# Loading the last 384 rows of three batches as fp32 through the SyncE queue beside the casting GpSimd queue

## The chip, the cores and the metric

One core of one Trainium2 chip. The metric is device time in microseconds, the median of several executions.

In the lines of the profile PE is TensorE, PEld its loading of weights, DVE VectorE, ACT ScalarE, POOL GpSimd and SP SyncE; q0 is the queue of the loads that GpSimd issues, q1 that of SyncE, and L75 is line 75 of the kernel. HBM is the memory outside the core, SBUF the one inside it. The rows "DMA" and "GB/s" cut the span in 40 slices: a digit is the busy share of the 16 DMA engines in tenths (9 is 90% or more), and GB/s is what they wrote.

## The reference

For each of 4 matrices of 4224 x 4224 fp32, the 2D prefix sum, its diagonal, and the running sum along that diagonal:

```python
def reference(x):
    ps = np.cumsum(np.cumsum(x, axis=1), axis=2)
    diag = np.diagonal(ps, axis1=1, axis2=2)
    return np.cumsum(diag, axis=1).astype(np.float32)
```

Every element of x counts, so 285.5 MB have to come from HBM; the result is 67 KB.

## The kernel before

Each batch is read as "strips": five of 768 rows (six rows per partition, `F2 = 6`) and a last one of 384 rows (three per partition, `F = 3`). All are cast from fp32 to bf16 by the load and share a pool of three buffers. The fourth batch cuts its end differently and is not changed.

```python
NBUF = 3
strips = ctx.enter_context(tc.tile_pool(name="strips", bufs=NBUF))

def strip_tile():
    return strips.tile([P, F2, N], BF16, name="strip")

def load_rows(o, b, r0):
    f = o.shape[1]
    nc.gpsimd.dma_start(
        out=o, in_=x[b, r0 : r0 + f * P, :].rearrange("(p f) w -> p f w", f=f))
# ... (cut)
def add_up(strip, f, r0, acc, ums, wp=0, ws=None):
    # TensorE sums the columns right of the diagonal block, straight from the strip
    for j in range(g + nw, NG):
        for q in range(f):
            columns(j, 0, GW, strip[:, q, j * GW : (j + 1) * GW])
    # ... (cut)
    for q in range(f):
        mu = mup.tile([P, F2 * P], BF16, name="mu")[:, : f * P]
        masked(mu, strip[:, q, r0:hi], ums[q], acc[:, q, 2:3])   # VectorE
        for h in range(nw):
            columns(g + h, 0, GW, mu[:, h * GW : (h + 1) * GW])  # TensorE
        if ws > wp:
            act_sum(acc[:, q, 0:1], strip[:, q, wp:ws])          # ScalarE
    row_sums(acc[:, :, 1], strip[:, :, ws:hi])                   # VectorE
# ... (cut) after the six-row strips of a batch:
        strip = strip_tile()
        if whole:                                   # batches 0, 1, 2
            load_rows(strip[:, :F], b, T0)
            add_up(strip[:, :F], F, T0, acc3[:, 0], um3)
```

## Time and profile before

| | before |
|---|---|
| time, median of the first 3 runs | 669.56 us |
| span of the profiled run | 667.0 us |
| busy: PE, VectorE, ScalarE, GpSimd | 32%, 50%, 21%, 4% |
| read from HBM | 285.47 MB, 428 GB/s over the span |
| loads through the GpSimd queue | 142.47 MB written (half of what is read) |

The table is read from the bottom: the two lines about bytes say what the kernel waits for, and the line of busy shares says that no compute engine comes near to that. The lines of the profile that carry this stand in the prediction.

### The profile page before, as it was taken

To read this page: it belongs to the slowest core of one execution; us is meant where nothing else is said; L and a number is where in the kernel's file an instruction comes from. 1 tells how busy PE (TensorE), PEld (TensorE's weight loads), DVE (VectorE), ACT (ScalarE), POOL (GpSimd) and SP (SyncE) were. 2 spreads that over 40 slices of the span, in tenths; PEclk is the share of its full clock that TensorE was granted. 3 is DMA by queue.
4 is the path that set the end of the run, shared out by engine and by line. 5 is a ranking of instruction groups with operands and counts; after the bars stand their busy time and mean duration, and the time that the engine had idled before them with its cause. 6 is when DMAs were issued, how large, how long until landed. Compare 5 with 4: busy or idle time off the path is not lost.

```text
span 667.0 us, 2828 instructions
## 1 busy us (share of the span) xinstructions
PE 215.1 (32%) x967; PEld 97.2 (15%) x967; DVE 336.3 (50%) x376; ACT 140.1 (21%) x225; POOL 27.0 (4%) x56
## 2 busy tenths in 40 slices
PE   0071522403118254140321633504032254250426
PEld 0030211101003022010110311201011122120202
DVE  2043617366924351745883415266398241635687
ACT  0001120406300103040630020304063002030436
POOL 5000000000000000000000000000000000001000
PEclk9995857666558586665655957567565586765758
DMA  9999999999999999999999999999999999999997
GB/s 203 219 219 219 218 219 219 217 217 216 208 215 219 219 219 217 216 219 219 219 219 215 216 211 217 220 219 216 216 216 219 220 215 218 216 215 219 216 207 144
DMA packets 7384, 143.25 MB, mean 215 GB/s; under 512 B 669, under 2 KB 842, under 8 KB 1866
## 3 DMA queue, kind: packets, MB, share of 16 engines
q0 software_dynamic: 7008, 142.47, 99.7%
q1 hardware_dynamic: 362, 0.61, 0.3%
q8 instruction: 7, 0.11, 0.1%
q14 instruction: 7, 0.06, 0.0%
HBM read 285.47 MB, written 0.07 MB: 428 GB/s over the span
## 4 chain that ended last, share of the span: by engine, by line
another core or an unknown queue 42%; DVE 25%; PE 23%; DMA 5%; issue 4%; DVEq 0%; POOLq 0%
PE d L198 23%; DVE acc L215 17%; DVE mu L218 7%; DMA strip<-in_x_dram 5%; PE fold L198 1%; DVE pu L215 0%; DVE c L397 0%; DVE c L218 0%; DVE tsum L215 0%; DVE acc L301 0%; DVE acc L304 0%; PE carry_ps L198 0%; DVE rows L331 0%; DVEq L218 0%
## 5 line engine op out<-in xcount | busy, mean ns | idle before, releaser
L218 DVE SCALAR_TENSOR_TENSOR mu<-strip,um 128x768 bf16<-128x768 bf16 (+1 forms) x129 | 110.7, 908 | 314.4 <-DMA strip<-in_x_dram 222.3
L198 PE MATMUL d<-strip,sel 128*11 128x384 bf16 x603 | 140.0, 406 | 344.4 <-DMA strip<-in_x_dram 344.4
L210 ACT ACTIVATE dump<-strip 128x416 bf16<-128x416 bf16 (+8 forms) x112 | 128.4, 1146 | 523.2 <-DMA strip<-in_x_dram 520.2
L215 DVE TENSOR_REDUCE acc<-strip 128x6 f32<-128x4608 bf16 (+6 forms) x23 | 195.9, 8518 | 0.0
L198 PEld LDWEIGHTS <-sel 128*11 128x11 bf16 x849 | 86.1, 101 | 526.3 <-issue 488.4
L198 PE MATMUL d<-mu,sel 128*11 128x384 bf16 x243 | 59.7, 355 | 67.5 <-DVE mu L218 67.4
L75 POOL DMA_DIRECT2D strip<-in_x_dram x24 | 16.5, 687 | 555.5 <-DVE acc L215 414.5
L210 ACT ACTIVATION_READ_ACCUMULATOR dump<-strip 128x1 f32 x112 | 20.9, 186 | 0.0
L218 DVE DVE_READ_ACCUMULATOR mu<-strip,um 128x1 f32 x129 | 10.6, 82 | 0.0
L198 PE MATMUL d<-ident,rows 128*11 128x128 f32 x24 | 5.2, 378 | 16.5 <-DVE rows L340 16.5
L198 PE MATMUL fold<-strip,ident_h 128*128 128x480 bf16 (+1 forms) x14 | 4.3, 458 | 8.4 <-DMA strip<-in_x_dram 8.4
L198 PE MATMUL d<-halves,rows 128*11 128x64 f32 x48 | 5.7, 304 | 0.0
L198 PEld LDWEIGHTS d<-halves,rows 128*11 128x11 f32 x48 | 5.1, 136 | 2.1 <-issue 2.1
L198 PEld LDWEIGHTS d<-ident,rows 128*11 128x11 f32 x24 | 2.6, 118 | 18.2 <-DVE rows L340 11.5
L215 DVE TENSOR_REDUCE pu<-d 11x1 f32<-11x384 f32 x4 | 2.2, 546 | 5.5 <-PE d L198 5.5
L397 DVE TENSOR_TENSOR_SCAN c<-ones_row,carry,c 11x384 f32<-11x384 f32 x4 | 4.0, 1006 | 0.1
L397 DVE TENSOR_TENSOR_SCAN c<-ones_row,carry,d 11x384 f32<-11x384 f32 x4 | 4.0, 1001 | 0.1
L198 PEld LDWEIGHTS <-ident_h 128*128 128x128 bf16 x20 | 2.2, 112 | 12.2 <-issue 11.8
L215 DVE TENSOR_REDUCE parts<-strip 128x3 f32<-128x3072 bf16 x1 | 3.4, 3350 | 0.0
L198 PE MATMUL d<-hmu,sel 128*11 128x384 bf16 (+2 forms) x3 | 0.7, 286 | 6.7 <-DVE hmu L218 6.7
L372 POOL DMA_DIRECT2D strip<-in_x_dram x2 | 1.4, 716 | 29.2 <-DVE acc L215 29.2
L215 DVE TENSOR_REDUCE tsum<-strip 128x1 f32<-128x384 bf16 (+2 forms) x3 | 1.7, 568 | 0.9 <-DMA strip<-in_x_dram 0.9
(78 smaller groups left out, 36.0 us busy)
## 6 DMA issues: line engine op xcount, KB each, us to landing
strip<-in_x_dram POOLq DMA_DIRECT2D x19, 6336.0 KB, 69.6
strip<-in_x_dram POOLq DMA_DIRECT2D x5, 3168.0 KB, 55.3
strip<-in_x_dram POOLq DMA_DIRECT2D x1, 1080.0 KB, 45.3
strip<-in_x_dram POOLq DMA_DIRECT2D x1, 768.0 KB, 48.2
head<-in_x_dram SPq DMA_DIRECT2D x1, 528.0 KB, 3.9
strip<-in_x_dram POOLq DMA_DIRECT2D x1, 448.0 KB, 51.1
strip<-in_x_dram POOLq DMA_DIRECT2D x1, 416.0 KB, 49.5
strip<-in_x_dram POOLq DMA_DIRECT2D x1, 160.0 KB, 51.4
```

The lines of the kernel that those rows point to most:

```text
L75: nc.gpsimd.dma_start(out=o, in_=x[b, r0 : r0 + f * P, :].rearrange("(p f) w -> p f w", f=f))
L198: nc.tensor.matmul(o, lhsT=lhsT, rhs=rhs, start=start, stop=False, skip_group_check=True)
L210: nc.scalar.activation(out=dump[:, :w], in_=src, func=ACT.Copy, accum_out=acc)
L215: nc.vector.reduce_sum(out=acc, in_=src, axis=AX.X)
L218: nc.vector.scalar_tensor_tensor(out=o, in0=i, scalar=1.0, in1=m, op0=ALU.mult, op1=ALU.mult, accum_out=acc,)
L372: nc.gpsimd.dma_start(out=part_a[:, :, c0:c1], in_=src_a[:, :, c0:c1])
L397: nc.vector.tensor_tensor_scan(out=c12[:, i, :], data0=ones_row, data1=src, initial=carry[:, i : i + 1], op0=ALU.mult, op1=ALU.add,)
```

## The change

A load that doesn't cast can be issued by SyncE, as these three are in the changed kernel. The three-row strip as fp32 has just the size of a six-row strip as bf16, so it fits the same buffers. The intent is to have these three loads run beside the GpSimd queue and not behind it.

```diff
-    def load_rows(o, b, r0):
+    def load_rows(o, b, r0, eng=nc.gpsimd):
         f = o.shape[1]
-        nc.gpsimd.dma_start(
+        eng.dma_start(
@@
-        strip = strip_tile()
         if whole:
-            load_rows(strip[:, :F], b, T0)
-            add_up(strip[:, :F], F, T0, acc3[:, 0], um3)
+            strip = strips.tile([P, F, N], FP32, name="strip")
+            load_rows(strip, b, T0, nc.sync)
+            add_up(strip, F, T0, acc3[:, 0], um3)
@@
         else:
+            strip = strip_tile()
```

## The prediction

> **What bounds the kernel now.** I read first the page's slices and DMA queues, because every strip is loaded from HBM once.
>
> ```profile
> DMA  9999999999999999999999999999999999999997
> GB/s 203 219 219 219 218 219 219 217 217 216 208 215 219 219 219 217 216 219 219 219 219 215 216 211 217 220 219 216 216 216 219 220 215 218 216 215 219 216 207 144
> q0 software_dynamic: 7008, 142.47, 99.7%
> q1 hardware_dynamic: 362, 0.61, 0.3%
> HBM read 285.47 MB, written 0.07 MB: 428 GB/s over the span
> ```
>
> The DMA row is at 9 in 39 of 40 slices: the 16 engines never pause. The GB/s row counts bytes written to SBUF. The GpSimd queue casts fp32 to bf16 on the way, so each byte written stands for two read: 219 GB/s written is 438 read. All of x is read once, 285.5 MB, and at about 434 GB/s that alone takes 658 us of the 667 us span.
>
> The windows view (busy time of PE, PEld, DVE, ACT and POOL with instruction counts, then clock, DMA share, GB/s) shows how idle the rest is:
>
> ```profile
> 100.00:150.00 50.00, 12.53 (x57) 5.43 (x55) 28.51 (x20) 9.81 (x16) 1.26 (x2) 0.66 1.01 218
> 300.00:400.00 100.00, 29.12 (x128) 13.44 (x128) 53.42 (x54) 20.52 (x30) 2.84 (x4) 0.59 1.01 216
> ```
>
> DMA share is 1.01 while VectorE, the busiest engine, is at 53 to 57%. The chain agrees. Its unnamed pieces are the loads that it can't follow:
>
> ```profile
> 125.25 5.72 PE d L198 x20
> ...
> 133.72 11.27 DVE acc L215
> 144.98 10.12 another core or an unknown queue
> ...
> 160.62 13.28 DVE acc L215
> ...
> 176.41 6.58 DVE acc L215
> ...
> 186.66 13.36 another core or an unknown queue
> 200.07 11.71 PE d L198 x56
> ```
>
> Strip 3 (counting from 0) lands at about 125.2 us, where PE starts. VectorE waits again until strip 4 at 155.2. ScalarE starts the three-row strip 5 of batch 0 at 170.14 (timeline), and strip 6, batch 1's first, starts at 200.07. A six-row strip (12.98 MB read) thus takes 29.9 us and a three-row strip (6.49 MB) 15.0, both 433 to 434 GB/s: the spacing of landings is the transfer time.
>
> Last, whether the queue comes near to running dry. GpSimd's timeline has the issues (start, duration, idle before it and what ended that):
>
> ```profile
> 115.10 0.56 POOL L75 DMA_DIRECT2D strip<-in_x_dram  x1 [30.14 <-DVE acc L215]
> 145.61 0.70 POOL L75 DMA_DIRECT2D strip<-in_x_dram  x1 [29.95 <-DVE acc L215]
> 174.52 0.72 POOL L75 DMA_DIRECT2D strip<-in_x_dram  x1 [28.21 <-DVE acc L304]
> 183.51 0.72 POOL L75 DMA_DIRECT2D strip<-in_x_dram  x1 [8.27 <-issue]
> 219.92 0.71 POOL L75 DMA_DIRECT2D strip<-in_x_dram  x1 [35.70 <-DVE acc L215]
> ```
>
> These are strips 5 to 9, each issued when the strip three before it has been used up (three buffers). At 145.6 the queue still holds work until 170.1, at 174.5 until 200.0: some 25 us of transfers are always waiting.
>
> **What the Trainium skill says.** "DMA: Bandwidth & Descriptors", Where 436 GB/s comes from: the ceiling is 16 SBUF ports of 32 B at 850 MHz, 435 GB/s, so 27.2 per engine. The trace agrees: in its packet records a cast packet of 25,344 B written (50,688 read) takes 1,886 ns and the next on that engine starts 1,867 ns after it, 27.15 GB/s of bytes read. The same page, Issuing engines are not separate DMA queues: transfers issued by SyncE and GpSimd run on the same 16 engines and interleave, and several issuers save only issue time. The trace before has no two large queues at once to test it. The same page, Queues, rings and completion order: each engine takes turns between the queues that have work, packet by packet; also untested here. "VectorE: DVE Perf Modes", The perf-mode tier table: tensor_reduce runs at 1x in bf16 and fp32 alike. The groups by form agree:
>
> ```profile
> L215 DVE TENSOR_REDUCE acc<-strip 128x3 f32<-128x6240 bf16 x3 | 19.9, 6647 | 0.0
> L218 DVE SCALAR_TENSOR_TENSOR mu<-strip,um 128x384 bf16<-128x384 bf16 x15 | 7.6, 554 | 1.8 <-DMA strip<-in_x_dram 1.7
> L215 DVE TENSOR_REDUCE hs<-head 128x2 f32<-128x1056 f32 x1 | 1.2, 1202 | 0.0
> L218 DVE SCALAR_TENSOR_TENSOR hmu<-head,um 128x384 bf16<-128x384 f32 x1 | 0.5, 534 | 0.0
> ```
>
> 6647 ns over 6240 bf16 elements is 1.07 ns each; 1202 over 1056 fp32 elements is 1.14 including the fixed part. The masked product of 384 columns took 554 ns from bf16 and 534 from fp32.
>
> **The change part by part.** *Bytes.* Three loads (batches 0 to 2) leave the casting queue. What is read from HBM is unchanged; what is written for them doubles, 9.73 to 19.46 MB (3 x 128 partitions x 50,688 B). Now they take 3 x 15.0 = 45 us of DMA time, 6.8% of the total. Does an uncast byte cost more? Cast packets fit 22 ns plus bytes read over 27.2 per ns: 286 ns for 7,168 read, 340 for 8,640, 1,886 for 50,688. The uncast packets in the same trace follow that line too: the runtime's 8,192 B packets have a median of 322 ns (the line gives 323), the 2,112 B packets of the SyncE-loaded head 86 (line: 100). So the engine's time goes by bytes read, and the three loads should keep 3 x 15 us: 0 us of change.
>
> *Issue.* GpSimd loses 3 of its 24 strip issues, about 0.7 us each; it is 4% busy and issues 25 us ahead: 0 us.
>
> *Compute.* On a three-row last strip (batches 0 to 2) there are three masked products, three ScalarE sums of 2,144 columns (1990 ns from bf16; no fp32 one exists in the trace) and one reduce of 6,240. No matmul reads the strip itself, since no column group lies right of it; PE reads only the bf16 product. By the pairs above VectorE stays at about 8.3 us per strip. If ScalarE stays at its rate too, 0 us; even a doubling would add 6 us to an engine that is 21% busy.
>
> *Order.* This is what really moves. Strip 5 is issued at 115.1 as before, but no longer stands behind strips 3 (10 us left) and 4 (30 us). With equal turns strip 3 lands near 135 instead of 125, strip 5 near 145 instead of 170, and strip 4 near 170 instead of 155; the sum, 10 + 30 + 15 us, ends at 170 either way. Strip 3's buffer then comes free 20 us after its landing, so strip 6 is issued near 156 (145.6 before) with 14 us of work still queued. Strip 4 is used up near 189, so strip 7 is issued near 190 (174.5 before) with strip 6 streaming until 200: 10 us left, the tightest point. Then VectorE does strip 5 (about 9 us) and the batch's end (5 us) by about 204, so strip 6 starts some 2 to 4 us late and strip 9 is issued near 223, with strip 7 and all of 8 ahead of it. The engines never run dry and the delay is gone before the next batch ends. 0 us.
>
> *End.* The last batch is untouched: the last load lands at about 661.3 us and 5.7 us of tail follow.
>
> Sum: 0 us, so 669.5.
>
> **The rivals.** First, uncast writes cost more. If an engine's time went by bytes written, the 45 us would double: about 714. If by read plus written (6 B per element cast, 8 uncast), a third more: +15, about 684. For it: no uncast packet of tens of KB has been seen, and its writes need the full 27.2 GB/s of a port that cast packets half use. Against: the 8,192 B packets on the same line. A small penalty of 5% would be +2 us, and I leave room for that.
>
> Second, the change of order starves the queue. If strip 3 or 4 landed so late that its successor was issued into an empty queue, each batch would lose the gap. For it: slack falls from 25 to 10 us by my schedule. Against: 10 us is still left, and it hardly depends on how turns are shared, since even if SyncE's transfer went wholly first, strip 3 would land at 140, strip 6 be issued at 160, and strip 4 still land at 170. A loss of up to 5 us per batch would make about 685 in the worst case.
>
> Third, two queues side by side fill holes and it gets faster. Packets on an engine already follow with 1,867 ns start to start against 1,863.5 at 27.2 GB/s, and dips such as slice 11's 208 GB/s add up to a few us, only a part of them near these loads: at best -3 us, about 666.
>
> **How the range and the chances follow.** All terms are zero because the bound resource moves the same bytes read at the same rate. The unknown is the large uncast packet (0 to +3 us likely, +15 unlikely) and the starvation (0 likely); on the other side at most -3. So 669.5, with 8 in 10 between 665 and 675. 2% is 13.4 us: gaining that would need more than the ceiling allows; losing it needs the first or second rival nearly in full.
>
> **What would show it.** Right: span near 667, HBM read 285.47 MB, q1 at about 20.1 MB and q0 at 132.7, DMA still 9 in every slice but the last, the GB/s row up (towards 330) in the slices where both queues run, SyncE's three loads landing some 30 us after issue, before the six-row strip issued ahead of them, and GpSimd issues for the next batch's first strips some 10 to 15 us later against the landings. The fp32 reduce stays near 6.6 us. Wrong: a slice with DMA under 9 (starvation), or full DMA with a later end (uncast packets slower than 15 us per strip), or a 6,240-element reduce or ScalarE sum much longer and strips waiting on it.

## The result, and the profile after

The changed kernel took 670.92 us (669.74 to 671.73, 6 runs), the kernel before 669.67 (668.67 to 670.19, 6 runs). The ratio is 1.0019, with an interval of 1.0006 to 1.0032. Within 2% this is the same time; whether the 1.25 us are real is the first question of the experiments.

The page of the changed kernel, the lines that answer to those in the prediction (its profiled run, 671.73 us, was the slowest of the six):

```profile
DMA  9999999999999999999999999999999999999995
GB/s 200 218 216 218 217 218 218 339 291 218 218 218 218 216 218 215 224 333 278 218 216 218 220 216 218 218 241 339 263 216 216 220 218 217 216 216 218 218 204 113
q0 software_dynamic: 6576, 132.74, 92.5%
q1 hardware_dynamic: 794, 20.07, 7.1%
HBM read 285.47 MB, written 0.07 MB: 426 GB/s over the span
```

DMA is at 9 in 39 of 40 slices, as before. q1, SyncE's queue, rose from 0.61 to 20.07 MB. The GB/s row has three new peaks of 333 to 339, one per changed load: there half of the engines' turns write 4 bytes per element and not 2. More is written, nothing more is read, and the DMA engines were and are busy throughout. A 9 could hide a gap of a tenth of a slice, 1.7 us; the packet records show none: between 6 and 655 us of both profiled runs all 16 engines always have a packet.

The order did change. The timelines of SyncE, GpSimd and PE (start, duration, and in brackets the idle time before) around the end of batch 0:

```profile
114.65 0.36 SPq L75 DMA_DIRECT2D strip<-in_x_dram  x1
```

```profile
153.01 0.71 POOL L75 DMA_DIRECT2D strip<-in_x_dram  x1 [65.85 <-DVE acc L215]
190.18 0.71 POOL L75 DMA_DIRECT2D strip<-in_x_dram  x1 [36.46 <-DVE acc L304]
199.17 0.71 POOL L75 DMA_DIRECT2D strip<-in_x_dram  x1 [8.27 <-DVE acc L304]
222.60 0.72 POOL L75 DMA_DIRECT2D strip<-in_x_dram  x1 [22.72 <-DVE acc L215]
```

```profile
133.43 4.60 PE L198 MATMUL d<-strip,sel 128*11 128x384 bf16 x18 [27.47 <-DMA strip<-in_x_dram]
170.80 2.08 PE L198 MATMUL d<-strip,sel 128*11 128x384 bf16 x6 [29.15 <-DMA strip<-in_x_dram]
202.25 11.86 PE L198 MATMUL d<-strip,sel 128*11 128x384 bf16 x54
```

SyncE issues strip 5 at 114.65. PE gets strip 3 at 133.4 (125.2 before) and strip 4 at 170.8 (155.2 before). In the packet records the data of strip 5 run from 118.0 to 146.6 us (its last completion is at 148.5), before strip 4, although strip 4 was issued 28 us earlier; on each engine one 50,688 B packet of SyncE's alternates with one of GpSimd's, each about 1,885 ns. Strips 6 and 7 are issued at 153.0 and 190.2 (145.6 and 174.5 before). Then the delay melts: PE begins strip 6 at 202.25, 2.2 us later than before, and strip 9 is issued 2.7 us later.

Compute cost nothing. The groups by form, the ScalarE sum before, which the prediction had not shown:

```profile
L210 ACT ACTIVATE dump<-strip 128x2144 bf16<-128x2144 bf16 x9 | 17.9, 1990 | 13.4 <-DMA strip<-in_x_dram 13.2
```

and after, all three kinds of work that now read fp32:

```profile
L215 DVE TENSOR_REDUCE acc<-strip 128x3 f32<-128x6240 f32 x3 | 19.9, 6647 | 0.0
L210 ACT ACTIVATE dump<-strip 128x2144 bf16<-128x2144 f32 x9 | 17.9, 1990 | 0.3
L218 DVE SCALAR_TENSOR_TENSOR mu<-strip,um 128x384 bf16<-128x384 f32 x9 | 4.5, 555 | 0.1
```

6647, 1990 and 555 ns against 6647, 1990 and 554: equal to a nanosecond. The idle time before the ScalarE sums fell from 13.4 to 0.3 us, because the strip is there early; ScalarE is no bottleneck, so this is worth nothing.

### The profile page after: what moved, and what is told of

Same layout as the page of the kernel before. It is cut to its first block, busy times and chain, and to the rows that moved or that the text cites. A ratio compares the mean times of both kernels' runs of the same rounds, so it can differ in the third digit from the quotient of the medians.

```text
span 670.0 us, 2832 instructions
## 1 busy us (share of the span) xinstructions
PE 216.2 (32%) x967; PEld 97.5 (15%) x967; DVE 336.1 (50%) x376; ACT 140.1 (21%) x225; POOL 25.3 (4%) x53
## 3 DMA queue, kind: packets, MB, share of 16 engines
q1 hardware_dynamic: 794, 20.07, 7.1%
## 4 chain that ended last, share of the span: by engine, by line
another core or an unknown queue 31%; DMA 31%; DVE 18%; PE 16%; issue 3%; POOL 0%; DVEq 0%; POOLq 0%
DMA strip<-in_x_dram 31%; PE d L198 15%; DVE acc L215 13%; DVE mu L218 5%; PE fold L198 0%; PE fin_b L198 0%; PE fin_a L198 0%; DVE tsum L215 0%; PE fold_a L198 0%; POOL strip L374 0%; DVEq L218 0%; DVE yl L448 0%; POOLq L75 0%; DVE hmu L218 0%
## 5 line engine op out<-in xcount | busy, mean ns | idle before, releaser
L218 DVE SCALAR_TENSOR_TENSOR mu<-strip,um 128x768 bf16<-128x768 bf16 (+2 forms) x129 | 110.6, 907 | 316.3 <-DMA strip<-in_x_dram 230.1
L75 POOL DMA_DIRECT2D strip<-in_x_dram x21 | 14.8, 708 | 559.5 <-DVE acc L215 397.0
L374 POOL DMA_DIRECT2D strip<-in_x_dram x2 | 1.4, 716 | 27.6 <-DVE acc L215 27.6
## 6 DMA issues: line engine op xcount, KB each, us to landing
strip<-in_x_dram SPq DMA_DIRECT2D x3, 6336.0 KB, 33.6
```

The costliest lines, as they stand in the source:

```text
L75: eng.dma_start(out=o, in_=x[b, r0 : r0 + f * P, :].rearrange("(p f) w -> p f w", f=f))
L218: nc.vector.scalar_tensor_tensor(out=o, in0=i, scalar=1.0, in1=m, op0=ALU.mult, op1=ALU.mult, accum_out=acc,)
L374: nc.gpsimd.dma_start(out=part_a[:, :, c0:c1], in_=src_a[:, :, c0:c1])
```

## The experiments

### Is the 0.2% real? The changed kernel again

Nothing was edited.

> The changed kernel unaltered, again. The first timing gave 1.0019 of before (0.0006 to 0.0032 above 1). Theory A (the 1.25 us are a scatter of the start and end of the load stream between runs, as in the profiled run, where two of the 16 DMA engines fell 1.3 us behind in the first strip and stayed behind): ratio between 0.999 and 1.002, interval touching 1, and the first strip lands anywhere between 34 and 36 us. Theory B (the second queue or the fp32 writes really cost 1 us or more): ratio again 1.0015 or more with an interval clear of 1.

669.67 us (669.22 to 670.20, 6 runs) against 670.05 for before (668.70 to 672.01, 11 runs): ratio 0.9995, interval 0.9980 to 1.0010. That is the ratio of theory A. The first piece of the chain of waits (start, duration, what), in the profiled run of the first timing and in that of this one:

```profile
1.33 34.54 DMA strip<-in_x_dram
```

```profile
1.32 33.24 DMA strip<-in_x_dram
```

The same program's first strip took 1.3 us longer in one run, long before any changed load. By the completion packets two of the 16 engines finished it at 35.3 and 35.6 us and the others by 34.5, and at the end two completions again came 1.1 and 1.9 us behind the rest. With no pause in the stream a lag of the start is not made good. So the profiled run's lag was there before the change could act. That the other five runs of the first timing were slower for the same reason is not shown; what is shown is that the excess did not come back. An effect under 0.1% stays open.

### The data type without the second queue

```diff
-            load_rows(strip, b, T0, nc.sync)
+            load_rows(strip, b, T0)
```

> The three last strips still land as fp32, but through the GpSimd queue, so in the old order. Theory A (engine time goes by bytes read; order hidden): about 669.7 us, ratio 0.999 to 1.002, landing order as before (three-row strip after the six-row one), its packets 50,688 B in about 1,885 ns. Theory B1 (fp32 writes cost): the same excess as the changed kernel's, 1.0015 or more. Theory B2 (the second queue costs): equal to before, with the changed kernel above it in the same rounds.

669.73 us (6 runs), ratio 0.9994 (0.9978 to 1.0011). The order is the old one: the fp32 strip takes no turns with another, so one slice of the GB/s row per load reaches 387 to 410, and strips 6 and 7 are issued at 144.5 and 174.4. Its 50,688 B packets took 1,874 ns on average. With the type alone changed here, and type and queue in the run above in the same rounds (0.9995), neither costs anything that shows.

### Loads alone, three ways

The compute is taken out (a wrong result): 44 three-row strips, one 64-element reduce on each, and a store of zeros and sums.

```diff
+    for i in range(B * NG):
+        b, g = i // NG, i % NG
+        cast = MODE == "cast" or (MODE == "mixed" and i % 2 == 0)
+        pool = pools["cast" if cast else "plain"]
+        strip = pool.tile([P, F, N], BF16 if cast else FP32, name="strip")
+        eng = nc.gpsimd if cast else nc.sync
+        eng.dma_start(out=strip, in_=...)   # ... (cut: the rows of strip g of batch b)
+        nc.vector.reduce_sum(out=acc[:, i : i + 1], in_=strip[:, 0, 0:64], axis=AX.X)
```

> Loads alone (wrong result on purpose): all of x in 44 three-row strips cast to bf16 through the GpSimd queue, three buffers, one 64-element reduce per strip. 285.47 MB at 434 GB/s is 658 us, plus about 4 us to the first byte and 3 to 5 at the end: 662 to 670 us. All theories agree; it is the measure for the next two.

> The same 44 strips as fp32 through the SyncE queue. Theory A (engine time goes by bytes read): within 1% of the cast kernel, 660 to 672 us, HW packets 50,688 B in about 1,885 ns. Rival 1 (by bytes written): about 1,315 us. Rival 2 (read plus written, 8 B against 6 per element): about 880 us. A small penalty of 5% on uncast bytes would show as 33 us.

> Strips alternate: even ones cast through GpSimd, odd ones fp32 through SyncE, two buffers each, so both queues are always in flight. Theory A: same 660 to 672 us; the two queues share, each strip takes about 30 us from first to last packet instead of 15. Rival 3 (two queues interfere, or fill each other's holes): over 1% longer or shorter than both pure kernels.

The times are 667.71, 668.10 and 668.03 us, 4 runs each (667.61 to 668.37 in all), with the whole kernel before at 668.98 in the same rounds. One line of the windows view for each, in the order cast, plain, mixed (stretch, its length, busy time of VectorE and GpSimd with counts, clock, DMA share, GB/s written):

```profile
300.00:400.00 100.00, 1.54 (x7) 3.69 (x7) 1.00 1.02 218
```

```profile
300.00:400.00 100.00, 1.54 (x7) 0.00 (x0) 1.00 1.01 437
```

```profile
300.00:400.00 100.00, 1.38 (x8) 2.11 (x4) 1.00 1.02 328
```

218 GB/s written with a cast is 436 read; 437 written without is 437 read; mixed, 328 is the mean of the two. The three times lie within 0.1% while the bytes written differ by a factor of two: with packets of this size the engines' time goes by the bytes read, at some 27 GB/s for each of the 16 (437 / 16). Both queues do share in the mixed kernel: a strip takes 26.9 us from its first packet to its last (some 30 were expected), and 16.1 to 16.4 in the pure ones. This refutes the rivals by bytes written (1,315 us) and by read plus written (880), and also that two queues disturb each other or fill each other's holes. It also bounds the whole kernel: with all its compute it is about 1 us slower than its loads alone.

### With the slack taken away: two strip buffers

```diff
-    NBUF = 3
+    NBUF = 2
```

in the kernel before,

> The kernel before with two strip buffers instead of three. My schedule model (30 us per six-row load, 15 per three-row, 19.7 us and 9 us from landing to release, 2.3 us from issue to first byte) has 25 us of queued loads with three buffers and runs dry only after each batch's three-row strip with two: about 21 us longer, 685 to 697 us, DMA slices under 9 once per batch. If order and slack don't matter (loads are simply bandwidth), it stays near 670.

in the changed kernel,

> The changed kernel with two strip buffers. Theory (turn-taking delays the strip issued ahead of the SyncE strip by up to 8 us, hidden only by the 10 us of slack that the third buffer gives): with that slack gone the delay shows, about 24 us more than two buffers before: 705 to 725 us, roughly 8 us per batch in three batches. Rival (the order change costs nothing even without slack, because the sum of transfers is the same): equal to the two-buffer kernel before, within 5 us.

and with two buffers and the fp32 strip through GpSimd, run after the two, on another chip (the kernel before took 669.47 us there, 670.05 beside the other two):

> Two strip buffers, the three last strips fp32 but through the GpSimd queue, so in order. The two-buffer kernel before took 693.9 us and the two-buffer changed kernel 716.7. Theory (the 23 us between them are the turn-taking of two queues): 692 to 696 us here. Rival (fp32 strips or their release are the cost once there is no slack): near 717 us.

Results: 693.87 us (692.73 to 696.07), 716.70 (714.62 to 717.78) and 694.95 (694.74 to 695.89), 4 runs each. The DMA row of the page and PE's start on strip 4, from the timeline; two buffers before:

```profile
DMA  9999999996999999999699999999969999999996
```

```profile
155.06 2.08 PE L198 MATMUL d<-strip,sel 128*11 128x384 bf16 x6 [21.09 <-DMA strip<-in_x_dram]
```

two buffers, changed:

```profile
DMA  9999999993799999999469999999955999999997
```

```profile
162.57 2.08 PE L198 MATMUL d<-strip,sel 128*11 128x384 bf16 x6 [28.70 <-DMA strip<-in_x_dram]
```

two buffers, fp32 in order:

```profile
155.07 2.08 PE L198 MATMUL d<-strip,sel 128*11 128x384 bf16 x6 [21.23 <-DMA strip<-in_x_dram]
```

Before, one slice per batch drops to 6: the queue runs dry once, after the three-row strip. In the changed kernel this grows to two slices per batch (3 and 7, 4 and 6, 5 and 5). The packet records give the size: from 6 to 680 us the engines stand idle for 22.0 us in all before and 45.4 changed, 23.4 more. Strip 4 lands 7.5 us later because it takes turns with the strip issued behind it: in batch 0, 15 engines complete it after three of SyncE's packets and one after four, 4 x 1.88 us, and a strip has landed only with its last engine. Three batches of that are 22.5 us, against 716.7 - 693.9 = 22.8 measured. With fp32 in order strip 4 is back at 155.07 and the time at 695, so turn-taking is the cost and not the type. The second queue does have a price; the third buffer hides it. The schedule model's absolute times were some 3 us short (21 us for two buffers before, 23.8 measured); the difference that it was asked for, 24 us, was close, in part by luck. The model had the first byte 2.3 us after an issue; SyncE's first packet came after 4.3 (149.1 against 144.7), so less of strip 4 was left to share than it thought. The extra whole packet on the last engine made up for that.

## Why the prediction was right

*The bound resource.* It said that the 16 DMA engines never pause and that their time goes by bytes read. The packet records of the kernel show the first and the loads-alone kernels the second: 667.7 to 668.1 us whatever is written. The line through the packet records (322 ns for 8,192 B) held for packets six times as large: 1,883 ns on average for 50,688 B, where it gives 1,886. One reading was weaker than it looked. The prediction set its 27.15 GB/s of bytes *read* beside the ceiling of the SBUF *ports* and found agreement, but through the ports a casting load moves only half of that (218 GB/s in the loads alone, in the time in which 437 passed uncast). The figures agree; that the ports hold the casting loads back is not shown, and no run here says what does.

*Issue and compute, 0 us.* GpSimd's strip issues went from 24 to 21 with no effect. The reduce and the product were argued from pairs in the trace; for ScalarE no fp32 sum existed, and the prediction only bounded it. It measured 1990 ns in both types.

*Order.* This was the step with the most numbers, and the trace bears them out: strip 3 at PE at 133.4 us (said 135), strip 5's data at 146.6 and its completion at 148.5 (145), strip 4 at 170.8 (170), issues of strips 6, 7 and 9 at 153.0, 190.2 and 222.6 (156, 190 and 223), the end of the batch's sums at 204.6 by SyncE's store (204). Strip 3 came somewhat earlier than said; SyncE's first packet started 3.4 us after its issue, so the sharing began later, which fits. Two of the signs it named were a little off: SyncE's loads landed 33.6 us after their issue (some 30), and strips 6 and 7 were issued 7.4 and 15.7 us later than before (some 10 to 15). That the delay is absorbed rested on 10 us of queued work at the issue of strip 7: it came at 190.2, and strip 6 completed at 198.4 to 200.3. The packet records without a gap show that it was enough, and the two-buffer pair shows what it hid.

*The rivals.* Costlier uncast writes and a gain from two queues are both refuted by the loads alone. Starvation is not wrong as a mechanism, it is only out of reach with three buffers: with two it costs 22.8 us more.

*The range.* 669.5 was predicted and 670.92 and 669.67 were measured in two timings. The room of up to +3 us for large uncast packets was not needed.

## What to carry to other kernels

Where the DMA engines are full already, as here, and stay so, moving a large load to another queue or dropping its cast changes neither the engines' time for it nor the total, as long as the bytes read stay the same; compare with a kernel of the loads alone before working on anything else. A second queue does change the order of landing: a later load overtakes an earlier one by taking turns, so count how many microseconds of transfers are queued at each issue and whether they cover the delay of what is needed first. A change that is free with three buffers may cost 3% with two.

## What the Trainium skill lacked or had wrong

- "DMA: Bandwidth & Descriptors", Where 436 GB/s comes from: the note there says that for transfers between HBM and SBUF the HBM side, about 358 GB/s, binds. As it stands that is too low for one core at work: loads here ran at 433 to 437 GB/s of bytes read through either queue. The page's own 16 MB measurement of 425 is on the side of these runs, and its note beside that measurement has the condition that the sentence lacks, both cores of the pair loading; no run here has two at work.
- "DMA: Bandwidth & Descriptors", Issuing engines are not separate DMA queues: it says that a second issuer saves only issue time. The turn-taking by packets, which the page has under Queues, rings and completion order, is borne out by the packet records; what neither section says is what it does to the order of landing: with two buffers the strip issued first landed 7.5 us later, and the kernel took 22.8 us more.
- No page that was read says whether a casting load goes by the bytes read or written: a packet of 25,344 B written from 50,688 read took 1,886 ns, an uncast one of 50,688 B 1,883. So the casting loads, which put only 218 GB/s through the SBUF ports, took as long as the uncast ones with 437 (667.7 and 668.1 us).
